# Conformer/GLA block on one core: the mixer's first weight casts stand one place later on ScalarE

## The chip, the core and the metric

The kernel runs on one NeuronCore of a Trainium2 chip. A core has engines that each work through their own queue in order: TensorE (PE: matmuls; PEld: its weight loads), VectorE (DVE), ScalarE (ACT), GpSimd (POOL) and SyncE (SP), which issues most DMAs. The engines meet at semaphores. The metric is the device time of one execution in microseconds (us): 934.87 is the median of three runs (934.66 to 935.77).

## The reference

One layer of a streaming encoder on 512 rows of 1024 values, all float32:

```python
h = h + 0.5 * _swiglu(_rmsnorm(h, ffn1_norm[i]), ffn1_w_in[i], ffn1_w_out[i])
z = _rmsnorm(h, mix_norm[i]) @ w_in[i]
conv_a, conv_gt, q, k, v, r, g_lr = jnp.split(z, SPLIT_POINTS, axis=-1)
y_conv = _conv_module(conv_a, conv_gt, conv_w[i], conv_b[i], conv_ln_g[i], conv_ln_b[i])
y_gla = _gla(q, k, v, r, g_lr, gate_w_up[i], gate_b[i], gla_norm[i])
h = h + jnp.concatenate([y_conv, y_gla], axis=-1) @ w_out[i]
h = h + 0.5 * _swiglu(_rmsnorm(h, ffn2_norm[i]), ffn2_w_in[i], ffn2_w_out[i])
gate = jax.nn.sigmoid(_rmsnorm(h, ple_norm[i]) @ ple_w_gate[i])
h = h + gate * (p[i] @ ple_w_proj[i])
```

A final RMS norm follows. `_swiglu` is `silu(gate) * up` between two products; the feed-forward width is 2816. "The first layer" below is the first feed-forward product pair, and "the mixer" is the part from `w_in` to `w_out`.

## The kernel before

**Products in three parts.** Each float32 operand is split into a high part (cast to float32r) and a low part (the rest), and a product is three matmuls: high by high, high by low, low by high. For a weight tile, ACT casts the loaded tile `wr` into `wh` (`high`), and DVE subtracts to make `wl` (`low`). `added` makes the low part in another way: ACT writes the rounded negative of `wr` in the low part's place (`act.mul(l3, r3, -1.0)`), and POOL issues a DMA that accumulates `wr` onto it; in the trace that is a CAST, an ACTIVATE and a DMA_DIRECT2D for each tile.

**Buffers.** Loaded tiles `wr` have six buffers of 512 KB, `wh` and `wl` six each. A load is issued by SP in program order and waits until its buffer is free, which means that the last reader is done: DVE's `wl` subtraction, or, with `added`, the landing of POOL's accumulates. Which buffer a load takes follows from the order in which the program stops using the buffers.

**The first layer.** It works through column pairs of `w_in` (pair 10 is the last) with units named m1, m2, m6, m7, m5, m4 and m3, each a group of matmuls and the work behind it. `drive` emits the units in order, with weight preparation some units ahead. In pair 10's last unit, m3, ACT copies half of the accumulator `pd` to a tile `g`, DVE adds the other half and scales it, ACT takes silu (`s`), DVE multiplies (`m`), ACT casts (`act`, high part) and DVE makes its low part; the last pieces of the second product read them. These pieces add to the residual `h`; ACT then writes `hg` (high part of the scaled `h`), DVE its low part, and both the sum of squares `sqacc`. The mixer's first column blocks (PE `ps<-hg,wa`) read `hg` and the weight parts `wa`; in PE's order the sum over `sqacc` (`ps<-ones,sqacc`) stands among them.

**The mixer's first weights.** Four tiles of `w_in` are prepared by `ahead` with `added` in halves (`wa`): two at the hook on m4 of pair 10, two at the hook ("last", 4), a piece of the second product. A hook runs right behind its unit's own instructions. Four more tiles (`wh` from `pair` loads) follow in the mixer's code.

**What sets the order.** The wrapper `Ordered` ties each ACT, DVE and PE instruction to the one emitted before it, so these queues keep the program's order. `in_order(True)` is called again where the mixer's code starts and begins a new tie, so that the scheduler can place instructions of the mixer's code among the first layer's last ones.

The lines of m3 that matter:

```python
o = tmp("g1")
act.copy(two(o), p.x[:, :, 0:HALF])
dve.tensor_tensor(out=two(o), in0=p.x[:, :, HALF:], in1=two(o), op=ALU.add)
```

Of the kernel before, what the change touches and what calls it, by code (L numbers as in the profile page):

```python
# [15 lines left out]
P = 128  # L16
SEQ = 512
D = 1024
DC = D // P
DFF = 2816  # L20
D_CONV = 512
# [41 lines left out]
def block_kernel(ctx: ExitStack, tc: tile.TileContext, a: dict, out: bass.AP):  # L63
# [26 lines left out]
    def bt2(dt=F32R, s="a"):  # L90
        t = big.tile([P, 2, SEQ], dt, tag="A", bufs=NA, name=nm(s))
        hi, lo = t[:, 0], t[:, 1]
        whole_of[id(hi)] = hi, t
        return hi, lo
# [133 lines left out]
    def raw(nk, ncol):  # L228
        return wp.tile([P, 1024], F32, tag="raw", bufs=6, name=nm("wr"))[:, :nk * ncol].rearrange(
            "p (k c) -> p k c", k=nk)  # L230

    def fetch(r3, src, k0, nk, c0, ncol):
        nc.sync.dma_start(out=r3, in_=src[k0 * P:(k0 + nk) * P, c0:c0 + ncol].rearrange("(k p) c -> p k c", p=P))

    def load(src, k0, nk, c0, ncol):
        r3 = raw(nk, ncol)
        fetch(r3, src, k0, nk, c0, ncol)
        return r3
# [16 lines left out]
    def added(w):  # L255

        h3, l3, r3 = w
        act.mul(l3, r3, -1.0)
        pool.dma_start(out=l3.bitcast(F32), in_=r3, accum_op=ALU.add)
        return w  # L260
# [10 lines left out]
    def ahead(src, c0, ncol):  # L271


        return [[added(w) for w in high4(load(src, 0, DC, c, P))] for c in range(c0, c0 + ncol, P)]

    def high4(r3):

        w = []
        for k in range(0, DC, 4):
            hi, lo = (t.rearrange("p (k c) -> p k c", k=4) for t in bt2(s="wa"))  # L280
            act.copy(hi, r3[:, k:k + 4])
            w.append((hi, lo, r3[:, k:k + 4]))
        return w
# [355 lines left out]
    def constants():  # L639
        _, cwrow, gwurow = made  # L640
        gwu = cp.tile([P, 2 * P], F32, name="gwu")
        act.copy(gwu, gwurow)
        cw = cp.tile([P, 4 * WIDTH], F32, name="cw")
        ps = aux()
        for c in range(4):
            pe.transpose(ps[:, c * WIDTH:(c + 1) * WIDTH], cwrow[:, c * P:(c + 1) * P], ident[:WIDTH, :WIDTH])
        dve.tensor_copy(cw, ps[:, 0:4 * WIDTH])
        mean = cp.tile([P, P], F32, name="mean")
        pool.memset(mean, 1.0 / D_CONV)
        m1, m2 = (bt(s="m1")[:, 0:4 * CH].rearrange("p (c t) -> p c t", t=CH) for _ in range(2))  # L650
        mask = cp.tile([P, 4, CH], I32, name="mask")
        pool.memset(m1, 1.0)
        pool.memset(m2, 1.0)
        pool.affine_select(out=m1, in_=m1, compare_op=ALU.is_gt, fill=0.0, base=0,
                           pattern=[[0, 4], [-1, CH]], channel_multiplier=1)
        pool.affine_select(out=m2, in_=m2, compare_op=ALU.is_gt, fill=0.0, base=-CH,
                           pattern=[[0, 4], [-1, CH]], channel_multiplier=1)
        pool.tensor_copy(mask[0:CH], m1[0:CH])
        pool.tensor_copy(mask[CH:P], m2[CH:P])
        nbias = cp.tile([P, 2], F32, name="nbias")  # L660
        for j in range(2):
            dve.tensor_scalar(nbias[:, j:j + 1], vec("gate_b", j), -1.0, None, ALU.mult)
        made[:] = cw, gwu, mean, mask, nbias
# [359 lines left out]
    w_in = a["w_in"][0]  # L1023
    w_ahead = []

    def sums_hooks(x, names, at):

        h = {}
        for name, key in zip(names, at):
# [6 lines left out]
                  ("h4", 1): lambda *_: [steps[4](), xb.split("t2")],  # L1036
                  ("h5", 1): lambda *_: [xb.split("t3"), w2.s12()]})
    hooks.update({("m5", 3): lambda *_: made[0](), ("m3", 3): lambda *_: constants(),
                  ("m4", 10): lambda *_: w_ahead.append(ahead(w_in, D_CONV, 2 * P)),
                  ("last", 4): lambda *_: w_ahead.append(ahead(w_in, 0, 2 * P))})  # L1040
    FAR = {("h5", 1): 3, ("m1", 2): 3}
    CASTS = {("h5", 1): 4, ("m1", 2): 4}
# [78 lines left out]
    rs, rsb = mid  # L1121
# [427 lines left out]
    for k in range(4):  # L1549
        for n in range(3):  # L1550
            w, ps = half[n]
# [329 lines left out]
    rs = norm.rows()  # L1881
# [98 lines left out]
```

## Time and profile before

| what | value |
|---|---|
| median of three runs | 934.87 us (934.66 to 935.77) |
| profiled execution | 934.95 us, its span 933.1 us |
| PE busy | 923.0 us (99% of the span) |
| DVE busy | 826.6 us (89%) |
| ACT busy | 509.7 us (55%) |
| POOL busy | 56.9 us (6%) |
| mean granted TensorE clock | 0.997 |
| DMA | 114.37 MB, mean 123 GB/s |

The span runs from the first to the last instruction; the execution's own time is 1.85 us longer. Times in rows are us from the span's start. A row of a timeline reads: start, duration, engine, line, operation, output<-inputs (buffer numbers left out), shapes, count, and in brackets the engine's idle time before it with what ended it. A releaser is inferred: of several awaited events, the last one. All compute instructions here have line L46, that of the wrapper, so the tiles' names tell them apart. q1 is the queue of SP's DMAs, q0 that of POOL's.

### The profile page before, as it was taken

Reading aid. Unit: us, or ns where it says so; the run is one execution under the profiler, and the core shown is the slowest. Engines: PE = TensorE matmul, PEld = TensorE weight load, DVE = VectorE, ACT = ScalarE, POOL = GpSimd, SP = SyncE. Lnnn points to the kernel's source line nnn. Section 1 sums busy time; section 2 is a strip of 40 time slices with the busy share of each in tenths; the row PEclk is TensorE's granted clock in tenths of the full one; section 3 lists DMA queues with packets and bytes.
Section 4 is the critical chain, followed back from the end, with each engine's and each line's share of the span. In section 5 each row is a group of like instructions: output and inputs, shape, how many; then the busy total and the mean of one; then the engine's idle time right before and its main releaser. Section 6 shows DMA issues by size and latency. Waiting matters only on the chain.

```text
span 933.1 us, 12990 instructions
## 1 busy us (share of the span) xinstructions
PE 923.0 (99%) x5011; PEld 785.3 (84%) x5011; DVE 826.6 (89%) x1107; ACT 509.7 (55%) x745; POOL 56.9 (6%) x74
## 2 busy tenths in 40 slices
PE   9999999999999999999999999999999999999996
PEld 7898888888888878788877889888888888888885
DVE  6799989999999776999987789999999999997896
ACT  5874445445544574463564875355445444456883
POOL 0100100000000021001030020000000000000131
PEclk9999999999999999999999999999999999999998
DMA  7643333233432594346552654333223422348463
GB/s 231 186 112 113 116 113 113 74 108 113 124 87 66 153 237 116 77 111 161 137 124 79 158 115 134 113 113 116 89 90 122 126 89 79 110 132 245 92 111 115
DMA packets 108129, 114.37 MB, mean 123 GB/s; under 512 B 5203, under 2 KB 96517, under 8 KB 108068
## 3 DMA queue, kind: packets, MB, share of 16 engines
q1 hardware_dynamic: 101748, 94.67, 33.0%
q0 software_dynamic: 6304, 18.88, 11.2%
q8 instruction: 39, 0.64, 0.3%
q14 instruction: 22, 0.18, 0.1%
q10 hardware_dynamic: 16, 0.00, 0.0%
HBM read 93.61 MB, written 2.10 MB: 103 GB/s over the span
## 4 chain that ended last, share of the span: by engine, by line
PE 96%; DVE 2%; ACT 1%; DMA 1%; issue 0%; POOLq 0%; DVEq 0%; ACTq 0%
PE ps L46 58%; PE pd L46 38%; DMA wr<-in_w_in 1%; DVE wl L46 1%; DVE sq L46 0%; DVE g L46 0%; ACT act L46 0%; ACT wa L46 0%; ACT wh L46 0%; DVE u L46 0%; DVE rs L46 0%; ACT yc L46 0%; DVE y L46 0%; DVE s L46 0%; DVE act L46 0%
## 5 line engine op out<-in xcount | busy, mean ns | idle before, releaser
L46 DVE TENSOR_TENSOR wl<-wr,wh 128x1024 fp32r<-128x1024 f32 (+2 forms) x161 | 188.6, 1182 | 18.6 <-ACT wh L46 18.5
L46 ACT CAST wh<-wr 128x1024 fp32r<-128x1024 f32 (+2 forms) x178 | 176.4, 1022 | 21.6 <-PE ps L46 6.4
L46 PE MATMUL pd<-hg,wh 128*128 128x512 f32 x576 | 150.0, 391 | 0.0
L46 PE MATMUL ps<-act,wh 128*128 128x512 f32 x448 | 138.8, 391 | 0.5 <-ACT act L46 0.3
L46 PEld LDWEIGHTS pd<-hg,wh 128*128 128x128 f32 x576 | 106.1, 188 | 20.7 <-DVE u L46 0.3
L46 PE MATMUL ps<-hg,wh 128*128 128x512 f32 (+1 forms) x448 | 117.7, 347 | 0.1
L46 PE MATMUL pd<-t,wh 128*128 128x512 f32 x392 | 98.3, 393 | 0.0
L46 PEld LDWEIGHTS ps<-act,wh 128*128 128x128 f32 x448 | 83.1, 188 | 17.7 <-ACT act L46 0.7
L46 ACT ACTIVATE s<-g 128x512 f32<-128x512 f32 x48 | 30.3, 632 | 117.7 <-DVE g L46 117.7
L46 ACT COPY sq<-pd 128x1024 f32<-128x1024 f32 x45 | 45.8, 1017 | 86.7 <-PE pd L46 52.4
L46 PEld LDWEIGHTS ps<-hg,wh 128*128 128x128 f32 x448 | 78.0, 190 | 11.7 <-issue 1.3
L46 PE MATMUL ps<-act,wl 128*128 128x512 f32 x224 | 87.2, 389 | 0.0
L46 PE MATMUL pd<-hg,wl 128*128 128x256 f32 (+1 forms) x544 | 83.9, 289 | 0.0
L46 PEld LDWEIGHTS pd<-hg,wl 128*128 128x128 f32 x544 | 75.9, 190 | 6.3
L46 PEld LDWEIGHTS pd<-t,wh 128*128 128x128 f32 x392 | 70.6, 189 | 12.5
L46 PE MATMUL ps<-hg,wl 128*128 128x512 f32 (+1 forms) x224 | 77.1, 344 | 0.0
L46 ACT CAST wh<-sm 128x1024 fp32r<-128x1024 f32 x42 | 44.1, 1051 | 57.1 <-DVE sm L46 50.9
L46 DVE SCALAR_TENSOR_TENSOR cv<-glu,cw,cv 128x502 f32<-128x502 f32 (+24 forms) x90 | 61.9, 734 | 0.3
L46 PEld LDWEIGHTS pd<-t,wl 128*128 128x128 f32 x392 | 53.5, 191 | 3.8
L46 DVE TENSOR_TENSOR sq<-pd,sq 128x1024 f32<-128x1024 f32 x45 | 54.8, 1219 | 0.8 <-PE pd L46 0.8
L46 DVE TENSOR_TENSOR wl<-sm,wh 128x1024 fp32r<-128x1024 f32 x42 | 51.1, 1220 | 5.0 <-ACT wh L46 5.0
L46 PE MATMUL ps<-wh,hg 128*128 128x512 f32 x176 | 54.8, 393 | 0.0
(322 smaller groups left out, 1638.5 us busy)
## 6 DMA issues: line engine op xcount, KB each, us to landing
wr<-in_ffn_w_in SPq DMA_DIRECT2D x84, 512.0 KB
wr<-in_ffn_w_out SPq DMA_DIRECT2D x32, 512.0 KB
wr<-in_w_in SPq DMA_DIRECT2D x20, 512.0 KB
wl<-wr POOLq DMA_DIRECT2D x18, 512.0 KB, 5.2
wr<-in_ffn_w_out SPq DMA_DIRECT2D x16, 384.0 KB
wr<-in_w_out SPq DMA_DIRECT2D x8, 512.0 KB
wq<-in_ple_w_gate SPq DMA_DIRECT2D x8, 512.0 KB
wl<-wq POOLq DMA_DIRECT2D x8, 512.0 KB, 4.6
```

What stands on the lines that cost most here:

```text
L46: inst = call(*args, **kwargs)
```

## The change

`ahead` is cut in two: the loads, and `prepared`, which makes the parts. At the hook on m4 of pair 10 only the two loads are issued; the two tiles are prepared at the hook on m3 of pair 10, one unit later, behind that unit's copy. The other use of `ahead` stays as it is.

```diff
     def ahead(src, c0, ncol):
-        return [[added(w) for w in high4(load(src, 0, DC, c, P))] for c in range(c0, c0 + ncol, P)]
+        return prepared([load(src, 0, DC, c, P) for c in range(c0, c0 + ncol, P)])
+
+    def prepared(rs):
+
+        return [[added(w) for w in high4(r3)] for r3 in rs]
...
-                  ("m4", 10): lambda *_: w_ahead.append(ahead(w_in, D_CONV, 2 * P)),
+                  ("m4", 10): lambda *_: w_ahead.append([load(w_in, 0, DC, D_CONV + i * P, P) for i in range(2)]),
+                  ("m3", 10): lambda *_: w_ahead.append(prepared(w_ahead.pop())),
                   ("last", 4): lambda *_: w_ahead.append(ahead(w_in, 0, 2 * P))})
```

What this makes of ACT's order at pair 10's last units. Before; `wr_528` and `wr_531` are the mixer's tiles, `g1_537` is the copy:

```order
L46 CAST wh_524_3000<-wr_507_2915 128x768
L46 CAST wa_529_3028<-wr_528_3026 128x512
L46 CAST wa_530_3030<-wr_528_3026 128x512
L46 ACTIVATE wa_529_3028<-wr_528_3026 128x512
L46 ACTIVATE wa_530_3030<-wr_528_3026 128x512
L46 CAST wa_532_3038<-wr_531_3036 128x512
L46 CAST wa_533_3040<-wr_531_3036 128x512
L46 ACTIVATE wa_532_3038<-wr_531_3036 128x512
L46 ACTIVATE wa_533_3040<-wr_531_3036 128x512
L46 CAST wh_535_3048<-wr_512_2942 128x768
L46 COPY g1_537_3068<-pd_495_2842 128x512
L46 CAST wh_538_3072<-wr_518_2972 128x768
```

After; the tiles are `wr_528` and `wr_529`, the copy is `g1_533`, and `s_540` is the silu of it:

```order
L46 CAST wh_524_3000<-wr_507_2915 128x768
L46 CAST wh_531_3032<-wr_512_2942 128x768
L46 COPY g1_533_3052<-pd_495_2842 128x512
L46 CAST wa_534_3056<-wr_528_3026 128x512
L46 CAST wa_535_3058<-wr_528_3026 128x512
L46 ACTIVATE wa_534_3056<-wr_528_3026 128x512
L46 ACTIVATE wa_535_3058<-wr_528_3026 128x512
L46 CAST wa_536_3064<-wr_529_3028 128x512
L46 CAST wa_537_3066<-wr_529_3028 128x512
L46 ACTIVATE wa_536_3064<-wr_529_3028 128x512
L46 ACTIVATE wa_537_3066<-wr_529_3028 128x512
L46 CAST wh_538_3072<-wr_518_2972 128x768
```

The eight mixer instructions moved behind a weight cast of the second product (`wh_531`) and the copy, and stay ahead of the next weight cast (`wh_538`) and of the silu.

SP's loads from the first mixer tile on, with the semaphores that each waits for (DMASW: POOL's accumulates have landed; DMAHW: an SP load; DVE and Activation: an instruction there). Before:

```order
L233 DMA wr_547_3127<-in_w_in 128x8x128 [waits DMASW3_49,DMAHW7_49,DMASW2_49,Activation_49]
L233 DMA wr_550_3137<-in_w_in 128x8x128 [waits DMAHW4_49,DVE_49]
L233 DMA wr_576_3301<-in_w_in 128x8x128 [waits DMAHW0_49,DMASW5_49,DMASW4_49]
L233 DMA wr_577_3303<-in_w_in 128x8x128 [waits DMAHW5_49,DVE_49]
L233 DMA wr_578_3305<-in_w_in 128x8x128 [waits DMAHW6_49,DVE_49]
L233 DMA wr_579_3307<-in_w_in 128x8x128 [waits DMASW7_49,DMAHW2_49,DMASW6_49,Activation_49]
```

After:

```order
L233 DMA wr_547_3127<-in_w_in 128x8x128 [waits DMAHW4_49,DVE_49]
L233 DMA wr_548_3129<-in_w_in 128x8x128 [waits DMASW3_49,DMAHW7_49,DMASW2_49,Activation_49]
L233 DMA wr_576_3301<-in_w_in 128x8x128 [waits DMAHW5_49,DVE_49]
L233 DMA wr_577_3303<-in_w_in 128x8x128 [waits DMAHW0_49,DMASW5_49,DMASW4_49]
L233 DMA wr_578_3305<-in_w_in 128x8x128 [waits DMAHW6_49,DVE_49]
L233 DMA wr_579_3307<-in_w_in 128x8x128 [waits DMASW7_49,DMAHW2_49,DMASW6_49,Activation_49]
```

No load moved, but the buffers changed hands: the third and the fourth mixer load have exchanged what they wait for, and so have the fifth and the sixth. DMASW2 and 3 are the accumulates of the first mixer tile, 4 and 5 those of the second, 6 and 7 those of the third (`wr_547`), for which `wr_579` waits both before and after.

A second place on ACT, where the first layer's last `hg` are made. `wh_589` is the cast of `wr_579`, for a mixer block whose turn on PE comes later; `hg_558` to `hg_563` are operands of the mixer's first block. Before:

```order
L46 CAST wh_584_3317<-wr_578_3305 128x1024
L46 ACTIVATE hg_558_3200<-h_7_104,vcol_145 128x512
L46 ACTIVATE hg_559_3203<-h_8_105,vcol_145 128x512
L46 ACTIVATE sq_560_3207<-h_7_104 128x512
L46 ACTIVATE sq_561_3210<-h_8_105 128x512
L46 CAST wh_589_3355<-wr_579_3307 128x1024
L46 ACTIVATE hg_562_3232<-h_9_106,vcol_145 128x512
```

After:

```order
L46 CAST wh_584_3317<-wr_578_3305 128x1024
L46 ACTIVATE hg_558_3200<-h_7_104,vcol_145 128x512
L46 CAST wh_589_3355<-wr_579_3307 128x1024
L46 ACTIVATE hg_559_3203<-h_8_105,vcol_145 128x512
L46 ACTIVATE sq_560_3207<-h_7_104 128x512
L46 ACTIVATE sq_561_3210<-h_8_105 128x512
L46 ACTIVATE hg_562_3232<-h_9_106,vcol_145 128x512
```

The cast moved up by three instructions, ahead of `hg_559`. The orders of PE and DVE are the same before and after.

## The prediction

> **What bounds the kernel now.** I read the page's busy shares first, then the chain of waits, then the timelines engine by engine around the place that the change touches, and last the DMA queues there.
>
> ```profile
> PE 923.0 (99%) x5011; PEld 785.3 (84%) x5011; DVE 826.6 (89%) x1107; ACT 509.7 (55%) x745; POOL 56.9 (6%) x74
> PE 96%; DVE 2%; ACT 1%; DMA 1%; issue 0%; POOLq 0%; DVEq 0%; ACTq 0%
> ```
>
> TensorE (PE) is busy 99% of the span and carries 96% of the chain that ended last. A move of ScalarE (ACT) work can only gain what PE waits for here, and can only lose by making PE wait. In order of time the chain leaves PE at the end of the first feed-forward layer; its rows there (start, us, what):
>
> ```profile
> 318.42 5.70 DMA wr<-in_w_in
> ...
> 324.67 1.67 ACT wa L46 x3
> ...
> 332.29 3.48 PE ps L46 x14
> ```
>
> Those three `wa` instructions are mixer casts. PE and its operand loads, same place:
>
> ```profile
> 330.91 0.39 PE L46 MATMUL ps<-act,wl 128*128 128x512 f32 x1
> 331.56 0.51 PE L46 MATMUL ps<-act,wh 128*128 128x512 f32 x1 [0.27 <-ACT act L46]
> 332.29 0.50 PE L46 MATMUL ps<-act,wh 128*128 128x512 f32 x1 [0.22 <-DVE act L46]
> 332.63 0.39 PE L46 MATMUL ps<-act,wl 128*128 128x512 f32 x1
> 332.86 0.63 PE L46 MATMUL ps<-act,wh 128*128 128x512 f32 x2
> ```
>
> In steady flow a matmul starts 0.23 us after the last one (332.63 to 332.86). Four steps from 330.91 would be 331.82; the fourth starts at 332.86. So this stall costs **1.04 us**, the most that the change can win here.
>
> Later PE is held again, by little, on the same layer's results:
>
> ```profile
> 356.33 1.68 PEld L46 LDWEIGHTS ps<-hg,wa 128*128 128x128 f32 x8 [0.36 <-DVE hg L46]
> 358.39 0.97 PEld L46 LDWEIGHTS ps<-ones,sqacc 128*128 128x128 f32 x8 [0.38 <-DVE sqacc L46]
> ```
>
> This decides the case: VectorE (DVE) finishes `hg` and `sqacc` with no time to spare. If PE comes 1 us earlier, it waits here 1 us longer, unless DVE's chain moves too; if DVE's chain comes later, PE does.
>
> **Step 1, the copy goes ahead of the casts.** ACT before:
>
> ```profile
> 318.84 1.14 ACT L46 CAST wa<-wr 128x512 fp32r<-128x512 f32 x2 [2.42 <-DMA wr<-in_w_in]
> 324.15 1.14 ACT L46 CAST wa<-wr 128x512 fp32r<-128x512 f32 x2 [3.11 <-DMA wr<-in_w_in]
> 325.19 1.15 ACT L46 ACTIVATE wa<-wr 128x512 fp32r<-128x512 f32 x2
> 326.25 0.82 ACT L46 CAST wh<-wr 128x768 fp32r<-128x768 f32 x1
> 326.97 0.57 ACT L46 COPY g<-pd 128x512 f32<-128x512 f32 x1
> 327.45 0.83 ACT L46 CAST wh<-wr 128x768 fp32r<-128x768 f32 x1
> 329.42 0.63 ACT L46 ACTIVATE s<-g 128x512 f32<-128x512 f32 x1 [1.14 <-DVE g L46]
> 330.89 1.14 ACT L46 CAST act<-m 128x512 fp32r<-128x512 f32 x2 [0.84 <-DVE m L46]
> 321.31 1.12 PE L46 MATMUL pd<-hg,wl 128*128 128x256 f32 x8
> 330.18 0.69 DVE L46 TENSOR_TENSOR m<-u,s 128x512 f32<-128x512 f32 x1
> ```
>
> The copy's accumulator is complete at 321.31 + 1.12 = 322.43, but ACT stands at a mixer load until 324.15. After: the `wh` cast runs in ACT's idle time before, the copy at 322.46 to 323.03. Four `wa` instructions take 2.10 (324.15 to 326.25), so the eight end at 327.15, and their loads (landed by 318.84 and 324.15) hold none of them. Then `wh` to 327.98 and `s` at 327.88, against 329.42. DVE has added and scaled `g` by 325.3; it makes the next `wl` from 328.01, `m` at 328.88 against 330.18 (its places 0.87 apart, as from 329.30 to 330.18). So `act` comes **1.30 us** earlier; PE needed 0.92 at the worst (332.29 against 331.37). The stall goes: 1.04 us for PE.
>
> **Step 2, the loads behind it.** Buffers change hands. The third mixer load takes the buffer that DVE frees after its `wl`: SP issues it at about 324.0, where now it waits for POOL's first two accumulates. The fourth takes the buffer that those two free; their sources are now made after 323, and POOL issues the four of the first two loads 1.97 behind the first cast of each four (324.15 to 326.12), at 324.9 and 327.0, not at 320.81 and 326.12.
>
> ```profile
> 320.81 1.78 POOL L46 DMA_DIRECT2D wa<-wr  x2 [204.20 <-ACT wa L46]
> 326.12 1.75 POOL L46 DMA_DIRECT2D wa<-wr  x2 [3.52 <-ACT wa L46]
> 333.46 1.14 ACT L46 CAST wa<-wr 128x512 fp32r<-128x512 f32 x2 [0.69 <-DMA wr<-in_w_in]
> 335.43 1.75 POOL L46 DMA_DIRECT2D wa<-wr  x2 [7.57 <-ACT wa L46]
> 314.96 0.37 SPq L233 DMA_DIRECT2D wr<-in_w_in  x1
> DMA to landing us min/median/max: 7.0/7.8/8.4
> 344.05 0.37 SPq L233 DMA_DIRECT2D wr<-in_w_in  x1
> ```
>
> The row on landing is of the four accumulates issued from 335.43 on; the last is the eighth mixer load of this place (`wr_579`), which waits for the first two of them. Two stretches of the DMA queues, 336 to 339 and 340 to 345 (q1 SP's loads, q0 POOL's accumulates; packets, MB, share):
>
> ```profile
> q1 hardware_dynamic: 1732, 0.87, 115.8%
> ```
>
> ```profile
> q0 software_dynamic: 539, 0.98, 108.0%
> q1 hardware_dynamic: 35, 0.02, 1.6%
> ```
>
> From 336 to 339 q0 moves nothing, though accumulates were issued at 335.43: both queues share full engines. A load of 0.524 MB takes 1.8 us at 0.87 MB in 3; an accumulate of 0.262 MB 1.33 us at 0.98 MB in 5. The load issued at 314.96 on free queues was there by 318.84, 3.9 us, 2.1 beside its 1.8 of data; I put half of that ahead of the data. After: one load from 325.1, four accumulates (5.3) to 332.2, four loads (7.2) to 339.4, four accumulates to 344.7, then `wr_579`. The fourth load lands near 335 (332.2 + 1.8 + 1.0); its four casts end at 337.1, where the next `wh` cast starts, 0.5 us earlier than now:
>
> ```profile
> 337.64 1.77 ACT L46 CAST wh<-wr 128x768 fp32r<-128x768 f32 x2
> 338.50 0.96 DVE L46 TENSOR_TENSOR wl<-wr,wh 128x768 fp32r<-128x768 f32 x1 [4.74 <-ACT wh L46]
> ```
>
> DVE runs from 338.50 to the last `sqacc` almost without a pause, so it would win 0.5 us, if nothing else came.
>
> **Step 3, the moved cast.** The order of ACT changes at a second place that the diff doesn't name: `wh_589`, the cast of `wr_579`, stands ahead of `hg_559` instead of three places behind it.
>
> ```profile
> 344.62 1.33 ACT L46 ACTIVATE hg<-h,vcol 128x512 fp32r<-128x512 f32 x2
> 348.36 1.05 ACT L46 CAST wh<-wr 128x1024 fp32r<-128x1024 f32 x1 [1.36 <-DMA wr<-in_w_in]
> 346.18 1.41 DVE L46 SCALAR_TENSOR_TENSOR hg<-h,vcol,hg 128x512 fp32r<-128x512 f32 x2
> L46 ACT ACTIVATE hg<-h,vcol x8: 708/714/725, 340.8 to 355.4; 128x512 fp32r<-128x512 f32 x8
> L46 DVE SCALAR_TENSOR_TENSOR hg<-h,vcol,hg x8: 745/748/752, 341.7 to 356.2; 128x512 fp32r<-128x512 f32 x8
> ```
>
> The cast waits for a DMA until 348.36, while `hg_559`, the second of the two at 344.62, had started by 345.25 (344.62 + 1.33 - 0.71). Now `hg_559`, two squares on ACT and, in DVE's row, the low half of `hg_559` (before at 346.18 + 1.41 - 0.75 = 346.84) and all that follows to `sqacc` queue behind that load. If it lands at L, the cast starts at L, `hg_559` 0.95 later, takes 0.71, and DVE starts 0.04 behind: L + 1.70. DVE's delay is L - 345.14.
>
> Bounds on L: if the accumulates land as long after their issue as now, they come as much sooner as the casts that feed them: `act` at 329.60, `wh` at 330.65, then the casts at 331.4 for 333.46, 2.1 us, and L = 348.36 - 2.1 = 346.3; if the full queues hold them as now, 348.4. By the queue sum q0 drains at 344.7 against 345 now, so L is nearest the upper end: **347.9**. DVE's delay is +2.8, with +1.2 and +3.3 as ends.
>
> PE loses the step-1 gain at `hg` and `sqacc`, and waits until 358.39 + 2.8. Behind it one piece of the chain is PE's alone for 160 us, so nothing gives this back:
>
> ```profile
> 343.93 160.08 PE ps L46 x956
> ```
>
> No instruction is added or removed; DVE's and PE's own orders are unchanged. **Sum:** -1.04 won at 331 and waited off again at 356, +2.8 at the `hg` chain: +2.8 net. The profiled execution took 934.95 (span 933.1 and 1.85 around it), 0.08 above the median 934.87. Forecast 934.87 + 2.8 = **937.7 us**, 0.3% slower.
>
> **Rivals.** (a) The load `wr_579` is in time. For L up to 344.6 the moved cast costs nothing, DVE keeps its 0.5 us lead, PE ends 0.5 earlier: 934.4. For it speaks that POOL's accumulates are issued 2.1 us earlier; against it the full queues and the measured 7.0 us at the least.
>
> [...]
>
> (b) Between: L from 344.6 to 346.3, 934.4 to 936.0. (c) The change doesn't do what it says: the second mixer load lands later than 325.0, or `m` still waits; PE keeps its stall, the rest as in step 3 or nothing: about 935 to 938. Against it, that load landed at 324.15 even beside accumulates that now come later. (d) The queues get worse: the fourth load now waits for accumulates issued 4 us later, a gap of some 1.5 us opens before the next four loads, and L is 350: +4.9, 939.7.
>
> **How the numbers follow.** Step 3 as forecast, L from 346.3 to 349: 0.64, with its own range 936.0 to 938.7. (a) 0.12, (b) 0.10, (c) 0.05, (d) 0.09. The range 934.8 to 939.0 leaves out (a), (d) and some of (b). A change of 0.2% (1.87 us) is about what a measurement of this kernel can tell from none. Slower by more needs L above 347.0: most of the forecast's cases, (d) and some of (c), 0.69. Faster by more would need over 1.87 us, where PE's stall and its two later waits hold about 1.3: 0.03. The rest, 0.28, is the same.
>
> **What would show it.** Step 1: the `g` copy near 322.5, no PE idle time at 331. Step 2: a mixer load issued near 324. Step 3: ACT idle from about 345.5 to 348 on a DMA, ahead of a `wh` cast that stands between two `hg`; DVE idle beside it; PE waiting some 3 us for `hg` and `sqacc` at 354 to 361. If that ACT wait is short, or ends before 344.6, the prediction is wrong.

## The result and the profile after

The changed kernel takes 939.5 us (median of 6, 938.11 to 940.61) against 934.61 (median of 6, 934.23 to 935.77) before: a ratio of 1.0051, 95% interval 1.0038 to 1.0064. It is slower, as forecast, by 4.9 us and not by 2.8, which is 0.5 us above the range. The profiled execution is the quickest of the six, 938.11 with a span of 936.3, or 3.16 more than the profiled execution of before.

The page of the changed kernel, its busy times and the chain that ended last:

```profile
PE 922.9 (99%) x5011; PEld 784.5 (84%) x5011; DVE 826.8 (88%) x1107; ACT 509.7 (54%) x745; POOL 56.9 (6%) x74
PE 92%; DMA 2%; DVE 2%; issue 2%; ACT 1%; POOL 0%; SPq 0%; POOLq 0%; ACTq 0%; DVEq 0%
```

The work is the same; PE's share of the chain fell from 96% to 92%.
PE at the place of the old stall (timeline: start, us, what):

```profile
330.96 0.39 PE L46 MATMUL ps<-act,wl 128*128 128x512 f32 x1
...
331.87 0.61 PE L46 MATMUL ps<-act,wh 128*128 128x512 f32 x2
```

The four steps from 330.96 to 331.87 are 0.91 us: the stall of 1.04 us is gone. Twenty microseconds later PE stands still, and stands longer:

```profile
354.31 4.76 PE L46 MATMUL ps<-hg,wa 128*128 128x512 f32 x19 [3.24 <-ACT hg L46]
...
361.43 0.72 PE L46 MATMUL ps<-ones,sqacc 128*128 128x1 f32 x5
```

In the kernel before, the last of these rows is:

```profile
358.40 1.05 PE L46 MATMUL ps<-ones,sqacc 128*128 128x1 f32 x8
```

So `ps<-ones,sqacc` starts 3.03 us later than before. ACT before, at the second place (its later rows are in the prediction):

```profile
339.87 1.05 ACT L46 CAST wh<-wr 128x1024 fp32r<-128x1024 f32 x1 [0.46 <-PE pd L46]
340.83 1.33 ACT L46 ACTIVATE hg<-h,vcol 128x512 fp32r<-128x512 f32 x2
...
343.67 1.05 ACT L46 CAST wh<-wr 128x1024 fp32r<-128x1024 f32 x1 [0.47 <-DMA wr<-in_w_in]
```

ACT after, between the two places:

```profile
322.52 0.59 ACT L46 COPY g<-pd 128x512 f32<-128x512 f32 x1 [4.90 <-PE pd L46]
...
327.91 0.63 ACT L46 ACTIVATE s<-g 128x512 f32<-128x512 f32 x1
329.63 1.14 ACT L46 CAST act<-m 128x512 fp32r<-128x512 f32 x2 [1.10 <-DVE m L46]
...
336.00 1.14 ACT L46 CAST wa<-wr 128x512 fp32r<-128x512 f32 x2 [2.39 <-DMA wr<-in_w_in]
...
338.10 1.77 ACT L46 CAST wh<-wr 128x768 fp32r<-128x768 f32 x2
342.06 1.05 ACT L46 CAST wh<-wr 128x1024 fp32r<-128x1024 f32 x1 [2.19 <-DMA wr<-in_w_in]
343.01 1.33 ACT L46 ACTIVATE hg<-h,vcol 128x512 fp32r<-128x512 f32 x2
...
346.36 1.05 ACT L46 CAST wh<-wr 128x1024 fp32r<-128x1024 f32 x1 [0.97 <-DMA wr<-in_w_in]
347.31 0.72 ACT L46 ACTIVATE hg<-h,vcol 128x512 fp32r<-128x512 f32 x1
348.16 1.05 ACT L46 CAST wh<-wr 128x1024 fp32r<-128x1024 f32 x1
349.12 0.71 ACT L46 ACTIVATE hg<-h,vcol 128x512 fp32r<-128x512 f32 x1
```

Three weight casts stand here ahead of `hg`, each in need of its load: that of `wr_577` starts at 342.06, with 2.19 us of idle time before it (339.87 in the kernel before), that of `wr_578` at 346.36 (before 343.67), and the moved one, of `wr_579`, at 348.16. So `hg_555`, the first of the `hg` here, is already 2.18 us late (343.01 against 340.83), ahead of the place where the moved cast stands; and when ACT comes to the moved cast, at 348.03, it hardly has to wait any more. The chain of waits runs through the accumulates of the third mixer tile and the load of `wr_579`:

```profile
333.92 7.75 DMA wa<-wr
...
341.81 6.25 DMA wr<-in_w_in
```

The DMA queues of the changed kernel in the two stretches that the prediction read, 336 to 339 and 340 to 345 (packets, MB, share of 16 engines):

```profile
q1 hardware_dynamic: 1112, 0.56, 65.7%
q0 software_dynamic: 147, 0.27, 49.5%
```

```profile
q0 software_dynamic: 353, 0.64, 69.7%
q1 hardware_dynamic: 1220, 0.62, 43.4%
```

Before, in the prediction's rows, the queues took turns: 0.87 MB of loads with no accumulate, then 0.98 MB of accumulates with next to no load. Now both move in both stretches.

### The profile page after: what moved, and what is told of

It is laid out like the page before. It is cut to its first block, busy times and chain, and to the rows that moved or that the text cites. A ratio compares the mean times of both kernels' runs of the same rounds, so it can differ in the third digit from the quotient of the medians.

```text
span 936.3 us, 12990 instructions
## 1 busy us (share of the span) xinstructions
PE 922.9 (99%) x5011; PEld 784.5 (84%) x5011; DVE 826.8 (88%) x1107; ACT 509.7 (54%) x745; POOL 56.9 (6%) x74
## 4 chain that ended last, share of the span: by engine, by line
PE 92%; DMA 2%; DVE 2%; issue 2%; ACT 1%; POOL 0%; SPq 0%; POOLq 0%; ACTq 0%; DVEq 0%
PE ps L46 56%; PE pd L46 36%; DMA wr<-in_w_in 1%; DMA wa<-wr 1%; DMA wr<-in_ffn_w_in 0%; POOL wa L46 0%; DVE hg L46 0%; ACT hg L46 0%; ACT wh L46 0%; DVE sqacc L46 0%; DVE wl L46 0%; DVE g L46 0%; SPq L566 0%; SPq L528 0%; DVE h L46 0%
```

## The experiments

**What the theories are.** The prediction's theory: the moved cast holds `hg_559` until `wr_579` has landed, and that is the whole price. The rival that the trace of after suggests: the loads `wr_577` and `wr_578`, which share the DMA engines with accumulates that are now issued beside them, hold ACT ahead of `hg` too. A second question is why the other executions are 0.9 to 2.5 us longer than the profiled one.

**The changed kernel again.** No edit.

> The changed kernel once more, for its trace where the granted clock is below 0.996. Theory: on top of the 3.2 us by which the hg chain comes later, PE's one idle stretch of 3.2 us ahead of the first mixer block drops the TensorE clock for a while in most executions; then 938 to 940.6 us, a granted clock of 0.994 to 0.995 in most, and a stretch behind 354 us with a clock well below 1.00 and matmuls at more than 0.23 us apart. Rival: the executions beyond 938.1 differ in when the loads land; then hg and sqacc are later by 1 to 2 us in this trace, and the clock is 1.00 up to the kernel's last 30 us.

Measured: 939.09 us (938.49 to 940.61), ratio 1.0052 (1.0039 to 1.0065). The five executions: 938.49 at a mean granted clock of 0.998, then 939.84 and 940.61 at 0.994, 939.09 and 939.00 at 0.995. The kernel before shows 0.997 or 0.998 in all its runs. In this trace PE stands from 350.99 to 354.71, 0.5 us longer than in the first. The level stands, and the longer executions have the lower clock. The trace is of the quickest execution and shows no drop of the clock at this place, so it settles nothing between the expectation's theory and its rival.

**The cast put back.** The cast of `wr_579` goes behind the fourth square, as in the kernel before; everything else is the change.

```diff
...
     w2a.append(high(raw_a[1]))
+    act.behind(act.latest, norm.squares[3])
```

> The change, with the cast of wr_579 put back behind the two squares, where it stands before the change. Theory: 0.85 us of the 3.2 is this cast's; the other 2.2 are the cast of wr_577 ahead of hg_555, whose load now waits for accumulates that are issued later. So hg_559 is 2.2 us later than before, PE's idle stretch is about 2.4 us and the clock keeps 0.997: 936.8 us. Rival, as the prediction had it (the cast of wr_579 is all of the delay): 934.3 us.

Measured: 938.28 us (937.92 to 938.92), ratio 1.0041 (1.0028 to 1.0055), 0.8 less than the changed kernel beside it (the two ranges overlap), with clocks of 0.995 to 0.997. ACT of this run:

```profile
342.80 1.05 ACT L46 CAST wh<-wr 128x1024 fp32r<-128x1024 f32 x1 [1.75 <-DMA wr<-in_w_in]
...
346.98 1.06 ACT L46 CAST wh<-wr 128x1024 fp32r<-128x1024 f32 x1 [0.85 <-DMA wr<-in_w_in]
347.94 1.33 ACT L46 ACTIVATE hg<-h,vcol 128x512 fp32r<-128x512 f32 x2
...
350.22 1.03 ACT L46 CAST wh<-wr 128x1024 fp32r<-128x1024 f32 x1
```

The moved cast is out of the way at 350.22, and the two casts ahead of it still stand on their loads, to 342.80 and 346.98 (0.47 of that is an offset of this whole trace: its `g` copy starts at 322.99). The difference of 0.8 is what the theory gave; the level is 1.5 above it, and the clock, expected at 0.997, is below that in four of the five executions. With the other changes in place, the place of this cast is not the main cause.

**The cast alone.** The kernel before, with only the cast of `wr_579` ahead of `hg_559`. DVE's subtraction for `wr_578`'s tile also moves, ahead of the low part of `hg_559`.

```diff
...
     w2a.append(high(raw_a[1]))
+    act.behind(marks[3], act.latest)
```

> The kernel before, with the cast of wr_579 alone moved ahead of hg_559; DVE's subtraction for wr_578 also comes ahead of the low half of hg_559, and fills a part of its wait. Theory: the loads land as before, the cast starts at 348.4, the low half of hg_559 at 350.1 for 346.84, of which 1.1 is filled by the subtraction: the chain 2.1 us later, PE idle for less than 2 us in one piece, clock 0.997, 936.7 us. Rival (the moved cast costs nothing by itself): 934.6 us.

Measured: 936.95 us (936.63 to 937.2), ratio 1.0027 (1.0017 to 1.0037), 2.5 above the 934.49 of its batch. ACT:

```profile
348.04 1.05 ACT L46 CAST wh<-wr 128x1024 fp32r<-128x1024 f32 x1 [3.08 <-DMA wr<-in_w_in]
348.99 0.72 ACT L46 ACTIVATE hg<-h,vcol 128x512 fp32r<-128x512 f32 x1
```

By itself the cast does what step 3 says: 3.08 us of ACT idle time, `hg_559` at 348.99, its low half at 349.74 against 346.84. The two prices do not add: 2.5 for the cast alone, 3.8 for the change without it, 4.6 for both in this batch. Both hold the same ACT queue over the same time.

**Half the change.** The first mixer tile is prepared at the old place, the second behind the copy.

```diff
-                  ("m4", 10): lambda *_: w_ahead.append([load(w_in, 0, DC, D_CONV + i * P, P) for i in range(2)]),
-                  ("m3", 10): lambda *_: w_ahead.append(prepared(w_ahead.pop())),
+                  ("m4", 10): lambda *_: w_ahead.append(ahead(w_in, D_CONV, P) + [load(w_in, 0, DC, D_CONV + P, P)]),
+                  ("m3", 10): lambda *_: w_ahead[0].extend(prepared([w_ahead[0].pop()])),
```

> Only the second mixer tile is prepared behind the copy; the first stays where the kernel before has it, so buffers, loads and the place of the moved cast are as before. Theory (PE's stall at 331 is real but is waited off again where PE needs h, hg and sqacc of VectorE): PE shows no idle step at 331, sqacc ends at 358.3 within 0.3 as before, the time is 934.2 to 934.6, the same as before. Rival (the stall is a gain of its own): 933.4 to 933.6. If the second tile's move alone disturbs the loads: VectorE's hg chain late and 935.5 or more.

Measured: 936.61 us (934.87 to 937.56), ratio 1.0019 (1.0011 to 1.0028). No stall at 331 and the cast of `wr_579` at its old place, but 2 us lost: not the theory's time, but the expectation's third case, that the second tile's move alone disturbs the loads. The theory had the buffers wrong: the fifth and the sixth mixer load still exchange what they wait for, so that `wr_577` and not `wr_576` waits for the second tile's accumulates. ACT, and the two queues from 341.5 to 345:

```profile
338.47 2.72 ACT L46 CAST wh<-wr 128x768 fp32r<-128x768 f32 x3
...
346.05 1.05 ACT L46 CAST wh<-wr 128x1024 fp32r<-128x1024 f32 x1 [2.58 <-DMA wr<-in_w_in]
```

```profile
q0 software_dynamic: 377, 0.71, 110.8%
q1 hardware_dynamic: 23, 0.01, 1.6%
```

The cast of `wr_578` waits 2.58 us while 23 packets of loads, 0.01 MB, go by in 3.5 us. From 336 to 340, 2128 packets of loads (1.07 MB) had gone by beside 34 of accumulates: by the packets' times the bulk of that load was in before accumulates filled the engines (110.8% above); its last packets were not. The kernel before has the same thing in small, from 340.5 to 343.3:

```profile
q0 software_dynamic: 308, 0.57, 111.5%
q1 hardware_dynamic: 15, 0.01, 1.3%
```

There the records of these packets, one by one (start us, bytes, ns), are 0.19 us apart, and one accumulate packet of 2 KB takes 0.18 us:

```
341.07  512  41
341.27  512  41
341.46  512  41
```

The last comes at 343.24, and the cast of `wr_578` starts at 343.67. So a load's last packets went by one in about the time of an accumulate packet, while accumulates took 111.5% of the 16 engines' span. How packets of the two queues follow each other on one engine no trace here shows.

**The accumulates out of the way.** Two runs. In the base the cast of `wr_579` stands behind the last square, the rest is the change:

```diff
...
     w2a.append(high(raw_a[1]))
+    act.behind(act.latest, norm.squares[7])
```

> The changed kernel with the cast of wr_579 behind the last square; loads and accumulates as in the changed kernel. It is the base for the run with later accumulates. Both theories: the cast of wr_577 still waits until about 342 and that of wr_578 until about 346, sqacc ends near 360 to 361, 937.5 to 938.5.

The other moves, on top of it, the negated copies of the third and fourth mixer tile, and with them their accumulates, behind a square of the last `hg` (`late_lows` makes them there):

```diff
...
-                  ("last", 4): lambda *_: w_ahead.append(ahead(w_in, 0, 2 * P))})
+                  ("last", 4): lambda *_: w_ahead.append([high4(load(w_in, 0, DC, i * P, P)) for i in range(2)]),
+                  ("rest", 6): lambda *_: late_lows(w_ahead[1])})
```

> As the run with the cast behind the last square, and the negated copies and accumulates of the third and fourth mixer tile moved behind the fourth square (about 347), so that queue q0 moves nothing while SP's loads of 330 to 342 are under way. Theory (each load's last packets take turns with the accumulates' packets on the same DMA engines): the cast of wr_577 starts by 340 and that of wr_578 by 343.7 with no DMA wait over 0.5, sqacc ends at 357.5 to 358.5, 933.8 to 934.8, 3 to 4 less than the base. Rival (the loads are late because they are issued late, at 334.2, whatever q0 does): the cast of wr_577 still starts after 341, and 937 or more.

Measured: the base 938.31 us (938.09 to 938.78), ratio 1.0038 (1.0026 to 1.0051); with late accumulates 935.79 (935.22 to 936.43), ratio 1.0010 (1.0001 to 1.0019). ACT of the base:

```profile
342.25 1.05 ACT L46 CAST wh<-wr 128x1024 fp32r<-128x1024 f32 x1 [2.41 <-DMA wr<-in_w_in]
...
346.53 1.05 ACT L46 CAST wh<-wr 128x1024 fp32r<-128x1024 f32 x1 [0.95 <-DMA wr<-in_w_in]
```

ACT of the second run (the copies came behind the sixth square, at 353.60, not behind the fourth):

```profile
340.63 1.05 ACT L46 CAST wh<-wr 128x1024 fp32r<-128x1024 f32 x1 [0.71 <-DMA wr<-in_w_in]
...
343.86 1.04 ACT L46 CAST wh<-wr 128x1024 fp32r<-128x1024 f32 x1
...
353.60 2.18 ACT L46 ACTIVATE wa<-wr 128x512 fp32r<-128x512 f32 x4
```

The cast of `wr_577` comes at 340.63 in place of 342.25, that of `wr_578` at 343.86 in place of 346.53. SP issues `wr_577` at 334.01 in the base and at 333.95 here, so the issue is not the difference; and ACT, which is rid of four copies here, stood idle in the base ahead of that cast. From 334 to 342 the accumulates' queue moved 0.54 MB in the base and nothing here; the loads' queue 1.72 and 2.27 MB. So 2.5 of the 3.5 us that the base lost come from sharing the DMA engines. Some 0.7 of the 2.5 comes by way of the clock (0.995 or 0.996 in the base, 0.997 or 0.998 here; its price is worked out below). The expectation gave 3 to 4 and the time of before; 0.9 is left: ACT still stands 0.71 us on the load of `wr_577`, which SP issues behind the second tile's accumulates, at 333.95 where the kernel before has 332.31.

**No accumulates for the first two tiles.** Their low parts by four DVE subtractions in place of four ACT copies and four DMAs. This also frees the buffers earlier (SP issues `wr_577` at 328.57), so it takes away the late issue and the sharing together:

```diff
-                  ("m3", 10): lambda *_: w_ahead.append(prepared(w_ahead.pop())),
+                  ("m3", 10): lambda *_: w_ahead.append([[low(w) for w in high4(r3)] for r3 in w_ahead.pop()]),
```

> The changed kernel with the low parts of the first two mixer tiles made by four VectorE subtractions in place of four ScalarE copies and four accumulates. Theory (the harm comes from the loads that queue with those late accumulates): the subtractions fit into VectorE's idle time at 325 to 328; the fourth mixer load is issued near 328 in place of 330.4; the cast of wr_577 stands no longer ahead of hg at 342 but is over by 339; wr_579 lands near 343 to 345, so the moved cast costs 0 to 0.5; time 933.4 to 934.6. Rival (the place of the moved cast costs by itself, whatever the queues): hg_559 low still near 349.7 and 936.5 to 938.

and the same with the cast of `wr_579` behind the last square:

> As the run with four VectorE subtractions, and the cast of wr_579 behind the last square. Theory: nothing that waits for a late load stands ahead of hg any more; sqacc ends 0.5 to 1.0 before 358.34, PE has lost its stall at 331; 933.4 to 934.0, faster than before. Rival (VectorE's added subtractions delay its chain as much as the loads gain): 934.4 to 936.

Measured: 934.48 us (933.99 to 935.27), ratio 1.0000 (0.9991 to 1.0009); and 933.82 (933.34 to 934.1), ratio 0.9990 (0.9981 to 0.9998). In the first the moved cast is the only one that still waits:

```profile
335.87 2.00 ACT L46 CAST wh<-wr 128x1024 fp32r<-128x1024 f32 x2
...
344.28 1.05 ACT L46 CAST wh<-wr 128x1024 fp32r<-128x1024 f32 x1 [1.71 <-DMA wr<-in_w_in]
```

The casts of the fifth load and of `wr_577` are through by 337.87, and `hg_559` low comes at 345.99. The second is bound by PE alone; its chain of waits, and PE's `sqacc` row:

```profile
342.89 29.30 PE ps L46 x135
```

```profile
357.01 0.95 PE L46 MATMUL ps<-ones,sqacc 128*128 128x1 f32 x8
```

Here the stall at 331 is gone and is not waited off again: `ps<-ones,sqacc` starts 1.39 us before its time in the kernel before. This time lies in the expected range. The gain of 0.1%, 0.8 us, is small; its interval does not hold 1, but it is under what a measurement here safely tells from no change. The first run lies in the expected range, at the time of before.

**PE kept busy.** The changed kernel with 24 transposes of the identity into a bank that nothing reads, in PE's order ahead of the first mixer matmul.

```diff
-                  ("last", 4): lambda *_: w_ahead.append(ahead(w_in, 0, 2 * P))})
+                  ("last", 4): lambda *_: w_ahead.append(ahead(w_in, 0, 2 * P)),
+                  ("rest", 7): lambda *_: kept_warm(24)})
```

> The change, with 24 more transposes of the identity on PE between the last first-layer matmul and the first mixer block, into a bank that nobody reads, where PE idles anyway. Theory: the hg chain is as late as in the changed kernel, but no idle stretch is left above 1 us, and the clock is 0.997 or more in every execution: 937.7 to 938.1 us, with executions within 0.5 us of each other. Rival (the rest of the loss has another cause than PE's idle stretch): 939 to 940 us, and as wide a spread as the changed kernel's.

Measured: 938.35 us (938.01 to 939.21), ratio 1.0042 (1.0030 to 1.0055), clock 0.997 or 0.998 in all five executions; 0.7 less than the changed kernel beside it. The two ranges overlap, so the 0.7 is less sure than the clock. PE:

```profile
350.49 2.78 PE L46 MATMUL pd<-ident 128*128 128x128 f32 x24
354.23 4.77 PE L46 MATMUL ps<-hg,wa 128*128 128x512 f32 x19 [0.96 <-DVE h L46]
```

The mixer starts at the same time (354.23 against 354.31), but the clock no longer falls, where nine of the changed kernel's eleven executions had 0.994 or 0.995. The time is 0.25 above the expected range, and the executions lie 1.2 us apart, not within 0.5.

**PE kept idle for longer.** Twelve DVE additions into an unread tile ahead of the `h` that PE waits for.

```diff
+                        if n == 4 and plain:
+                            idle = tmp("idle", SEQ // 2, bufs=1)
+                            for _ in range(12):
+                                dve.tensor_tensor(out=idle, in0=hT[0][:, 0:SEQ // 2], in1=hT[1][:, 0:SEQ // 2], op=ALU.add)
                         add_to(0)
```

> The changed kernel with twelve VectorE additions of 128x256 into an unread tile ahead of the h for which PE waits at 351: PE's idle piece grows from 3.2 to some 7.5 to 8 us. Theory (a PE idle long enough makes the granted TensorE clock drop afterwards, and in the changed kernel's slower runs it has just done so): the trace shows a piece at half clock behind that idle, the clock of every run is 0.995 or less, and the time is that of the profiled run of the changed kernel, 938.1, plus 4.2 to 4.8 for the additions plus 1 to 2: 943.3 to 945. Rival (the lower clock has nothing to do with that idle): no such piece in the trace, clock 0.997 to 0.998, and 942.3 to 943.

Measured: 945.37 us (943.9 to 946.34), ratio 1.0112 (1.0098 to 1.0125), clock 0.990 to 0.993. The trace has the drop. A window of it (us; busy and count of PE, PEld, DVE, ACT, POOL; granted clock, DMA share, GB/s), and PE:

```profile
356.00:363.00 7.00, 3.50 (x8) 2.81 (x9) 6.57 (x13) 2.39 (x5) 0.00 (x0) 0.51 0.01 2
```

```profile
359.50 8.02 PE L46 MATMUL ps<-hg,wa 128*128 128x512 f32 x27 [8.34 <-DVE h L46]
```

The additions put `h` off by 5.39 us (352.68 to 358.07) and not by 4.2 to 4.8, the time is 0.4 above the expected range, and the clock's part is as the theory has it. The base with the cast behind the last square shows the same drop with no added work; three windows of that run, 3.4 us each, and PE's row:

```profile
350.80:354.20 3.40, 0.88 (x4) 0.48 (x3) 3.21 (x5) 1.25 (x3) 0.00 (x0) 0.99 1.12 283
354.20:357.60 3.40, 3.40 (x9) 2.63 (x8) 3.30 (x6) 1.57 (x4) 0.00 (x0) 0.50 0.30 110
357.60:361.00 3.40, 3.40 (x16) 2.82 (x15) 2.82 (x5) 2.87 (x5) 0.00 (x0) 1.00 0.00 0
```

```profile
353.65 7.99 PE L46 MATMUL ps<-hg,wa 128*128 128x512 f32 x27 [2.52 <-DVE h L46]
361.48 0.95 PE L46 MATMUL ps<-ones,sqacc 128*128 128x1 f32 x8
```

For 3.4 us, from 354.2 on, the clock is half, nine matmuls go by where sixteen do in the next window, and PE reaches `sqacc` 0.76 us after DVE has finished it (360.72), where the changed kernel's profiled execution came 0.06 after. So one such drop costs about 0.7 us here, as an estimate from these two traces, since some of it lies beside DVE's own lateness. The transposes made a difference of the same size.

## Why the prediction was right and wrong

Two steps failed. Step 2 let loads and accumulates have the DMA engines in turn and followed only one load to its cast, and so missed a part of the cause; and the sum had no term for the clock, which is what took the time out of the range.

**Step 1, right.** Copy at 322.52 (322.46 predicted), silu at 327.91 (327.88), `act` at 329.63 (329.60), no stall at 331. That the gain is lost again held too, though for the most part at another place than `hg` and `sqacc` (see below).

**Step 2, wrong.** The issues came as worked out (SP at 324.03, POOL at 324.98 and 327.06), and the fourth load landed near 336 where 335 was said. What failed is the queue sum, which let four loads and then four accumulates have the engines to themselves. They ran side by side; and the sum was only followed to `wr_579`. It took DVE to be 0.5 us early, because the `wh` cast at 337.1 would be; it came at 338.10, and the next two casts, of `wr_577` and `wr_578`, which I didn't follow to their loads, waited until 342.06 and 346.36. The run with late accumulates gives 2.5 us for this sharing, its effect on the clock included; the later issue of `wr_577` (334.22 for 332.31) belongs to it too, and no run takes that alone.

The row for it stood in the prediction: "35, 0.02, 1.6%" from 340 to 345. I read it as an empty queue. By its packets it is the tail of a load, drawn out to 343.24 at 0.19 us a packet; accumulates moved 0.98 MB in these 5 us. Every load in flight beside an accumulate had to be priced, not only the last. That does not explain why, in the kernel before, accumulates issued at 335.43 moved nothing until 339.7; that stays open.

**Step 3, right in its figures, wrong as the whole cause.** The load landed for a cast at 348.16 (L = 347.9), DVE's low half came 3.03 late (2.8). But without the moved cast 2.2 to 2.5 of it would have been there already, by `hg_555` and by DVE's rows of the two runs with the cast farther back, so putting the cast back returned 0.8. Alone, on the kernel before, the cast costs 2.5, near the 2.8.

**Where PE waits.** The prediction had PE wait in small pieces at `hg` and `sqacc`, 354 to 361. It waits in one piece of 3.2 us at the first mixer matmul, which starts 0.15 us after DVE's last-but-two addition to `h` ends (354.16 here, 359.35 in the run that kept PE idle for longer), and then 0.3 at `hg`, as it did before. That it waits for this addition to have read its accumulator is inferred: the row above names ACT's `hg`, which ends at the same time, the rows of the runs with transposes and with additions name DVE's `h`. The sum is the same, the effect isn't: behind one piece of 2.52 us, in the base with the cast behind the last square, the clock was 0.50 for 3.4 us.

**The sum, wrong by the clock.** The profiled execution has +3.16 where 2.8 was said. That is luck: the delay that step 2 overlooked hardly adds to the one that step 3 priced, because the two overlap. The median has 4.9, and the prediction put nothing down for the clock. The eleven executions of the changed kernel sort by it: 938.11 and 938.49 at 0.998, four from 939.00 to 939.21 at 0.995, five from 939.80 to 940.61 at 0.994. The two that kept the clock lie inside the range, and so does the median with PE kept busy, 938.35. Of the 1.7 between the two differences, 0.3 is how far the profiled execution of before lies above its median. About 0.7 of the other 1.4 is one drop of the clock; the rest isn't settled. An estimate from the traces: a piece of 3.4 us at half clock takes 0.0018 off the mean, and the end of each trace, where PE has no work left and the clock is half too (from 933.0 in the first trace of after, from 927.0 in the kernel before), takes off up to 0.0033. A mean of 0.994 needs more than both. So five executions probably had a longer stretch at half clock than the traced one; but no trace is of one, and whether their loads landed later as well isn't known (those of the two traces differ by 0.4).

**The rivals.** None of the four held. Rival (d), worse queues, was nearest with 939.7, but it had `wr_579` at 350, where it landed at 348.1. None of them has the clock.

## What to carry to other kernels

When a change shifts when DMAs are issued, follow every load that lands near them to the instruction that waits for it, not only the one whose wait you can see: a queue with a few packets in several microseconds need not be idle; here 35 packets in 5 us were a load's tail beside 0.98 MB of accumulates. An instruction that waits for a load should not stand ahead of work on the critical path of an in-order engine, but moving it back helps little if something else ahead of it waits as well: here it returned 0.8 of the 4.6 us. And look at the shape of PE's new idle time: here a single piece of 2.52 us was followed by 3.4 us at half clock, which cost some 0.7 us more by the estimate above.

## What the runs showed of the hardware

In the base with the cast behind the last square, an idle piece of 2.52 us was followed by 3.4 us at half TensorE clock (0.50), which began some 0.5 us after PE had started again (353.65, 354.2). Pieces of 3.24 and 3.73 us, in the two traces of the changed kernel, were followed by none (1.00 up to 365). Mean clocks of a kernel's executions, by the idle piece in its trace: 0.997 to 0.998 at 1.0 and 1.4 us, 0.996 to 0.998 at 1.7, 0.994 to 0.998 at 2.5 to 3.7, 0.990 to 0.993 at 8.3. What decides whether the clock drops behind such a piece, the runs do not show.

Accumulates of 256 KB took 3.9 to 7.8 us from issue to landing in the changed kernel.
